# Two hybrid encoder layers: the decay mask on POOL, and reciprocal head norms issued ahead of their products

## The chip, the cores and the metric

The kernel runs on one core of a Trainium2 chip. The metric is the device time of one execution in microseconds (us), as the median of several runs. The engines are TensorE (PE, with its weight load PEld), VectorE (DVE), ScalarE (ACT), GpSimd (POOL) and SyncE (SP, which issues the DMAs here). Each engine works through its own instructions strictly in order and waits on semaphores for the others.

## What is computed

The reference runs two DeepNorm layers on x of 512 tokens by 1024 channels. A layer projects x once for three branches, merges them by gates and projects the sum back.

- **State space (SSD).** 32 heads in 4 groups, two directions, chunks of 128 tokens. A depthwise convolution over 5 taps acts on the inputs x, B and C. In each chunk the output is a product with a decay matrix, `decay = exp(where(lower, a_cum[q] - a_cum[s], -inf))`, added to what the earlier chunks left in the state; it is gated with SiLU(z) and normed.
- **Differential attention.** 8 heads, two softmax maps each, `A1 - lambda*A2` times V, then an RMS norm per head, `y * rsqrt(mean(y*y) + 1e-5) * w`, and a SiLU gate.
- **Cross attention** into 256 memory tokens, with a gate.

All of it is float32; the kernel splits float32 operands into a high and a low part, and makes three TensorE passes of each product.

## The kernel before, in words

Everything is laid out as channels on 128 partitions and 512 tokens along the row. Weights come in units of 128 x 1024: a DMA (`wr`), a high part on ACT (`wh`), a low part on DVE (`wl`), then 24 matmuls of 128x512 into a `pj` bank (8 slices of x, three passes each). A plan lists the jobs; a scheduler then orders the instructions of each engine by priorities. `late(n)` shifts the priority of what is issued inside it: a positive n later, a negative one earlier. A second device, a manual schedule on PE alone, keeps PE's instructions as written there.

**SSD (`ssd`, lines 416 to 634).** For each of the four groups the plan holds the B and C parts (projection, convolution, and for B a transpose `pt<-bC`), four x parts, the states, and then for each quarter b = 0 to 3 a z part and a y part. The B part of the next group follows straight after the y part of b = 3. A y part (line 500) does for each of its two heads:

- a DMA brings the cumulated exponents of both directions to all partitions, `ab` (512 KB; two buffers in all);
- line 524 puts the mask on them with VectorE, `min`, over 128 x 1024;
- ACT takes the exponential, eight instructions of 128x128, each with its own bias;
- DVE adds the two directions (`ab<-ab`) and multiplies with the B-C product of the group: `m<-ab,gs`;
- PE multiplies `m` with the transposed x (`pm<-m,xsT`, eight products for two heads, which are sixteen entries in the trace).

DVE then adds the inter-chunk part to `y`, multiplies with `sz` and splits y into `yh` (ACT) and `yl` (DVE). ACT squares it into `sz`, and POOL adds that to `sqa` (the only work that POOL has here, besides two memsets). The convolution (`conv`, line 400) begins with one ACT instruction that reads the projection's bank (`acc<-pj`), goes on with four DVE instructions (`acc<-pj,hcw,acc`), a tanh on ACT (`th<-acc`) and ends on DVE (for B: `bC<-th,acc`).

**Differential attention (`diff`, lines 785 to 1026).** 35 units are walked through with a step counter s = 0 to 34; nst = 32, and the last units are gates. At step s PE has the unit's 24 matmuls in two halves of 12, and around them the scores of step s + 1, the turning of step s, and the values. After the last head's values (s = 32) `sums` (PE, s = 33) makes the sum of squares of head 7, which ACT copies to `ss`. The function `norm` then makes the reciprocal norms on DVE: a reciprocal, three small operations, the `rsqrt` by Newton steps (twelve small operations, last written tile `rs_y`) and a product, all on 128x4 for one head. `norms` does this for heads 0 to 6 at s = 30 and sends the result through PE and ACT to DRAM (`rd`). `last` does it for head 7 in the middle of s = 33 and multiplies `rs_y` with an identity on PE, which spreads it over the partitions (`pm<-cst,rs_y`). `fin(h)` fetches a head's norms as a broadcast DMA (`fth<-rd`, two buffers; for head 7 it reads the `pm` bank), multiplies `sdy`, and splits the product into `dy` (ACT high part, DVE low part). Two heads are finished after each step from s = 31 on. After that `branch_out` multiplies `dy` with the output weights (24 matmuls for each of its units, `pj<-dy`).

Of the kernel before, what the change touches and what calls it, by code (L numbers as in the profile page):

```python
# [15 lines left out]
ALU = mybir.AluOpType  # L16
# [4 lines left out]
P = 128  # L21
S = 512
D = 1024
KC = D // P
NL = 2
M = 256
EPS = 1e-5
# [14 lines left out]

LX, LD = 70, 80

FILL = (0, 2, 0, 2, 0, 4, 0, 0)

# [3 lines left out]
def bc(ap, shape):  # L52
    return ap.broadcast_to(shape)


class Net:
# [359 lines left out]
    def ssd(self, l):  # L416
        nc = self.nc
# [78 lines left out]
        def ypart(g, b):  # L496
            def f():
                sp = self.sp
                if b == 0:
                    self.yh = self.t(sp, [P, 4, S], "yh", F32R)  # L500
                    self.yl = self.t(sp, [P, 4, S], "yl", F32R)

                eb = self.t(sp, [P, 2, S], "eb", bufs=2)
                for hh in range(2):
                    h = g * 8 + 2 * b + hh
                    src = self.deb.rearrange("(d h) q -> h d q", d=2)[h:h + 1]
                    nc.sync.dma_start(out=eb[hh * 64:(hh + 1) * 64], in_=src.broadcast_to([64, 2, S]))
                for d, cs in ((0, (1, 2, 3)), (1, (0, 1, 2))):
                    ps = self.bank(self.pm, "pm")
                    for c in cs:  # L510
                        q = slice(c * P, (c + 1) * P)
                        self.mm(ps[:, q], self.prev[d, c][:, b * P:(b + 1) * P], self.cC[:, q])
                    q = slice(cs[0] * P, (cs[2] + 1) * P)
                    self.tt(eb[:, d, q], ps[:, q], eb[:, d, q], ALU.mult)

                py = self.bank(self.pm, "pm")
                ms = []
                for hh in range(2):
                    h = g * 8 + 2 * b + hh
                    ab = self.t(sp, [P, 2, 4, P], "ab", bufs=2)  # L520
                    src = self.dab.rearrange("(d h) q -> h d q", d=2)[h:h + 1]
                    nc.sync.dma_start(out=ab.rearrange("p d c q -> p d (c q)"), in_=src.broadcast_to([P, 2, S]))

                    self.tt(ab, ab, bc(self.msk[:, :, None, :], [P, 2, 4, P]), ALU.min)
                    for d in range(2):
                        for c in range(4):
                            j = 32 * d + h
                            self.act(ab[:, d, c, :], ab[:, d, c, :], AF.Exp, bias=self.bias[:, c, j:j + 1])
                    self.tt(ab[:, 0], ab[:, 0], ab[:, 1], ALU.add)
                    m = self.t(sp, [P, 4, P], "m", bufs=3)  # L530
                    self.tt(m, ab[:, 0], self.gs, ALU.mult)
# [253 lines left out]
    def diff(self, l):  # L785
        nc = self.nc
# [131 lines left out]

        def norm(lo, hi):

            n = 4 * (hi - lo)
            s0, ss = self.s0[:, 4 * lo:4 * hi], self.ss[:, 4 * lo:4 * hi]
            nc.vector.reciprocal(out=s0, in_=s0)
            self.stt(ss, ss, 1.0 / 128.0, s0, ALU.mult, ALU.mult)
            self.tt(ss, ss, s0, ALU.mult)
            self.ts(ss, ss, EPS, ALU.add)
            r = self.rsqrt(self.fp, ss, n)
            self.tt(r, r, s0, ALU.mult)
            return r

        def norms():

            n = 4 * (KC - 1)
            r = norm(0, KC - 1)
            pt = self.bank(self.pt, "pt")
            self.tr(pt[:n, :P], r)
            rt = self.t(self.fp, [n, P], "rt", bufs=1)
            self.act(rt, pt[:n, :P])
            self.rd = self.t(self.dp, [n, P], "rd")
            nc.sync.dma_start(out=self.rd, in_=rt)  # L940

        def last():

            r = norm(KC - 1, KC)
            self.rb = self.bank(self.pm, "pm")
            for c in range(4):
                self.mm(self.rb[:, c * P:(c + 1) * P], bc(r[:, c:c + 1], [P, P]), self.ident)
# [12 lines left out]
        def step(unit, *parts):  # L960

            def f(wh, wl):
                g = fn(wh, wl)
                for p in parts:
                    for job in p:
                        job()
                    next(g, None)
            fn, u = unit
            self.T(f, u)

        def job(fn, *a):
            return lambda: fn(*a)
# [17 lines left out]
        nst = 4 * KC  # L990
        for s, unit in enumerate(units):
            first = [job(scores, s + 1)] if s + 1 < nst else []
            amid = []
            if s % 4 == 2 and s < nst:
                amid.append(job(values, s // 4, 0))
            if s % 4 == 0 and 0 < s <= nst:
                amid.append(job(values, s // 4 - 1, 1))
            if s < nst:
                amid.append(job(turn, s))
            if s % 4 == 1 and 1 < s <= nst + 1:  # L1000
                first.append(job(sums, s // 4 - 1))
            if s == nst - 2:
                amid.append(norms)
            if s == nst + 1:
                amid.append(last)
            step(unit, first, amid)
            if s >= nst - 1:
                for h in range(2 * (s - nst + 1), min(2 * (s - nst + 1) + 2, KC)):
                    self.T(job(fin, h))
        self.T(order.close)  # L1010
        mgs = ([], [])

# [216 lines left out]
```

## Time and profile before

| | |
|---|---|
| runs | 2237.81, 2241.68, 2244.03 us; median 2241.68 |
| the profiled execution | 2240.25 us, its span 2238.5 us |
| granted TensorE clock, mean | 0.994 |
| PE busy | 2173.2 us (97%) |
| DVE busy | 1589.9 us (71%) |
| ACT busy | 1004.6 us (45%) |
| POOL busy | 52.9 us (2%), 38 instructions |
| DMA | 283.79 MB, 127 GB/s |

A page's times are those of the one profiled execution. A row of the timeline gives the start, the duration, the engine and line, output and inputs, the shape, how many equal instructions were put together (x), and in square brackets how long the engine stood idle just before and what ended that. Matmuls overlap: a 128x512 matmul lasts 0.39 us, but the next one starts 0.23 us after it.

SSD of layer 0 lies at about 50 to 500 us, that of layer 1 at about 1200 to 1650 us. The end of the differential attention lies at about 1014 us and 2129 us.

### The profile page before, as it was taken

The page shows a single profiled execution, that of the slowest core. Times are in us where ns is not written, and L with a number is a line of the kernel's source. Part 1 is how long each engine was busy: PE and PEld are TensorE (multiplying, and loading weights), DVE is VectorE, ACT ScalarE, POOL GpSimd, SP SyncE. Part 2 cuts the span into 40 slices and gives each one's busy share as a digit, 9 for nine tenths or more (in the row PEclk, how much of TensorE's full clock was granted, in tenths as well). Part 3 has the DMA queues.
Part 4 walks back from the last instruction along what each step waited for, and adds up shares of the span by engine and source line. Part 5 has one row for each costly group of instructions (what it writes and reads, how often), then busy time and mean ns, then how long its engine had stood idle before and what let it go on. Part 6 is the DMA issues. An engine that isn't in the chain of part 4 may idle for free.

```text
span 2238.5 us, 30344 instructions
## 1 busy us (share of the span) xinstructions
PE 2173.2 (97%) x11714; PEld 1787.8 (80%) x11714; DVE 1589.9 (71%) x2468; ACT 1004.6 (45%) x1895; POOL 52.9 (2%) x38
## 2 busy tenths in 40 slices
PE   8999999999999999998999999999999999999898
PEld 6777877788888788877996777787788887888678
DVE  7887888758544777765567888888744547777657
ACT  5664545424432555442355564554423325544430
POOL 0000000000000000000000000010100000000000
PEclk9999999999999999999999999999999999999999
DMA  4654444425453222233564545453433332223333
GB/s 148 180 160 144 147 142 138 126 85 190 145 179 115 90 81 82 81 104 108 163 225 115 165 141 151 132 152 122 123 124 118 116 106 85 78 84 90 109 99 128
DMA packets 108278, 283.79 MB, mean 127 GB/s; under 512 B 12588, under 2 KB 17252, under 8 KB 107876
## 3 DMA queue, kind: packets, MB, share of 16 engines
q1 hardware_dynamic: 108132, 281.84, 41.2%
q8 instruction: 92, 1.51, 0.3%
q14 instruction: 54, 0.44, 0.1%
HBM read 255.55 MB, written 17.85 MB: 122 GB/s over the span
## 4 chain that ended last, share of the span: by engine, by line
PE 71%; DVE 14%; DMA 7%; ACT 5%; issue 2%; SPq 0%; POOL 0%; DVEq 0%; POOLq 0%; ACTq 0%
PE pj L103 59%; PE pm L103 9%; DMA ab<-dab 4%; DVE wl L81 2%; PE pt L111 2%; DVE ab L81 2%; DVE acc L84 2%; ACT ab L91 1%; ACT wh L91 1%; DVE y L81 1%; DVE rx L81 1%; PE pt L103 1%; DMA wr<-wu 1%; DMA fth<-rd 1%; DVE yl L84 1%
## 5 line engine op out<-in xcount | busy, mean ns | idle before, releaser
L103 PE MATMUL pj<-xh,wl 128*128 128x512 f32 x1664 | 669.1, 402 | 10.8 <-DVE wl L81 8.9
L103 PE MATMUL pj<-xh,wh 128*128 128x512 f32 x1664 | 660.8, 397 | 0.0
L103 PE MATMUL pj<-xl,wh 128*128 128x512 f32 x1664 | 658.1, 395 | 0.0
L81 DVE TENSOR_TENSOR wl<-wr,wh 128x1024 fp32r<-128x1024 f32 x330 | 404.5, 1226 | 108.3 <-ACT wh L91 107.5
L91 ACT ACTIVATE wh<-wr 128x1024 fp32r<-128x1024 f32 x330 | 347.4, 1053 | 235.3 <-PE pj L103 199.5
L103 PEld LDWEIGHTS pj<-xh,wl 128*128 128x128 f32 x1664 | 314.1, 189 | 90.8 <-issue 18.3
L103 PEld LDWEIGHTS pj<-xh,wh 128*128 128x128 f32 x1664 | 313.7, 189 | 71.6 <-issue 6.0
L103 PEld LDWEIGHTS pj<-xl,wh 128*128 128x128 f32 x1664 | 314.1, 189 | 63.5 <-issue 3.6
L91 ACT ACTIVATE ab<-ab,bias 128x128 f32<-128x128 f32 x512 | 160.7, 391 | 121.9 <-DVE ab L81 121.3
L84 DVE SCALAR_TENSOR_TENSOR acc<-pj,hcw,acc 128x510 f32<-128x510 f32 x192 | 142.4, 743 | 23.8 <-ACT acc L91 22.4
L91 ACT ACTIVATE fpp<-pm,fmx 128x512 f32<-128x512 f32 x128 | 87.9, 687 | 83.4 <-DVE fmx L881 82.6
L881 DVE TENSOR_REDUCE fmx<-pm 128x1 f32<-128x512 f32 x128 | 87.0, 686 | 45.4 <-PE pm L103 45.1
L103 PE MATMUL pj<-yl,wh 128*128 128x512 f32 x256 | 102.3, 400 | 0.8 <-DVE yl L84 0.8
L103 PE MATMUL pj<-yh,wh 128*128 128x512 f32 x256 | 103.1, 403 | 0.0
L81 DVE TENSOR_TENSOR ab<-ab,cst 128x1024 f32<-128x1024 f32 x64 | 86.3, 1349 | 22.9 <-DMA ab<-dab 22.8
L103 PE MATMUL pj<-dy,wh 128*128 128x512 f32 (+1 forms) x384 | 101.9, 354 | 0.0
L103 PE MATMUL pj<-yh,wl 128*128 128x512 f32 x256 | 101.9, 399 | 0.0
L103 PE MATMUL pj<-cy,wh 128*128 128x512 f32 x256 | 78.8, 389 | 0.0
L103 PEld LDWEIGHTS pj<-dy,wh 128*128 128x128 f32 x384 | 68.0, 189 | 10.0
L103 PE MATMUL pj<-wh,xl 128*128 128x256 f32 x256 | 74.8, 292 | 0.0
L103 PE MATMUL pj<-wl,xh 128*128 128x256 f32 x256 | 72.4, 283 | 0.0
L103 PE MATMUL pj<-wh,xh 128*128 128x256 f32 x256 | 72.3, 283 | 0.0
(273 smaller groups left out, 3387.3 us busy)
## 6 DMA issues: line engine op xcount, KB each, us to landing
wr<-wu SPq DMA_DIRECT2D x336, 512.0 KB, 3.6
ab<-dab SPq DMA_DIRECT2D x64, 512.0 KB, 5.7
eb<-deb SPq DMA_DIRECT2D x64, 256.0 KB, 4.8
mkv<-dkv SPq DMA_DIRECT2D x16, 512.0 KB, 4.3
rsw<-rx SPq DMA_DIRECT2D x128, 64.0 KB, 2.0
dgt<-tg SPq DMA_DIRECT2D x18, 256.0 KB, 2.6
dkv<-mo SPq DMA_DIRECT2D x16, 256.0 KB, 4.0
dkv<-q SPq DMA_DIRECT2D x16, 256.0 KB, 3.7
```

The costliest lines, as they stand in the source:

```text
L81: (eng or self.nc.vector).tensor_tensor(out=out, in0=a, in1=b, op=op)
L84: self.nc.vector.scalar_tensor_tensor(out=out, in0=a, scalar=s, in1=b, op0=op0, op1=op1)
L91: self.nc.scalar.activation(out=out, in_=a, func=f, **kw)
L103: self.nc.tensor.matmul(out=out, lhsT=a, rhs=b, start=first, stop=last)
L111: self.nc.tensor.transpose(out=out, in_=x, identity=self.ident)
L881: nc.vector.tensor_reduce(out=mx[:, c:c + 1], in_=ps, axis=AX.X, op=ALU.min)
```

## The change

Two edits.

1. The mask of the exponents, 64 instructions of 128 x 1024, moves from VectorE to GpSimd, and `min` becomes `add`.
2. In `diff`, `norm` is now a job of its own, with an earlier priority (`late(-300)`). For heads 0 to 6 it stands after step 29 and its result is spread at s = 30 as before. For head 7 it stands after step 33, and the product with the identity moves from the middle of s = 33 to the middle of s = 34. The `fin` jobs are dealt out otherwise: heads 0 and 1 after s = 32, heads 2 to 4 after s = 33, heads 5 to 7 after s = 34.

```diff
-LX, LD = 70, 80
+LX, LD, LN = 70, 80, 300
...
-                    self.tt(ab, ab, bc(self.msk[:, :, None, :], [P, 2, 4, P]), ALU.min)
+                    self.tt(ab, ab, bc(self.msk[:, :, None, :], [P, 2, 4, P]), ALU.add, nc.gpsimd)
...
         def norm(lo, hi):
-            n = 4 * (hi - lo)
             s0, ss = self.s0[:, 4 * lo:4 * hi], self.ss[:, 4 * lo:4 * hi]
-            nc.vector.reciprocal(out=s0, in_=s0)
...
-            r = self.rsqrt(self.fp, ss, n)
-            self.tt(r, r, s0, ALU.mult)
-            return r
+            with self.late(-LN):
+                nc.vector.reciprocal(out=s0, in_=s0)
...
+                self.r = self.rsqrt(self.fp, ss, 4 * (hi - lo))
+                self.tt(self.r, self.r, s0, ALU.mult)
-        def norms():
+        def spread():
             n = 4 * (KC - 1)
-            r = norm(0, KC - 1)
             pt = self.bank(self.pt, "pt")
-            self.tr(pt[:n, :P], r)
+            self.tr(pt[:n, :P], self.r)
...
         def last():
-            r = norm(KC - 1, KC)
+            r = self.r
...
             if s == nst - 2:
-                amid.append(norms)
-            if s == nst + 1:
+                amid.append(spread)
+            if s == nst + 2:
                 amid.append(last)
             step(unit, first, amid)
-            if s >= nst - 1:
-                for h in range(2 * (s - nst + 1), min(2 * (s - nst + 1) + 2, KC)):
-                    self.T(job(fin, h))
+            if s in (nst - 3, nst + 1):
+                self.T(job(norm, *((0, KC - 1) if s < nst else (KC - 1, KC))))
+            for h in {nst: (0, 1), nst + 1: (2, 3, 4), nst + 2: (5, 6, 7)}.get(s, ()):
+                self.T(job(fin, h))
```

The scheduler orders more than the edited lines. The first place is PE in layer 0, where group 1 ends and group 2 begins. `pm_1922` takes the products of the last quarter, `pj_2075` is the projection that follows, and `bC_1977` is group 2's convolved B. Before:

```order
L103 MATMUL pj_2075<-xl_83,wh_1973 128x512
L103 MATMUL pj_2075<-xh_82,wh_1973 128x512
L111 MATMUL pt_2012<-cst_81,bC_1977 128x128 x4
L103 MATMUL pj_2075<-xh_82,wl_1974 128x512
L103 MATMUL pj_2075<-xl_83,wh_1973 128x512
```

and in the changed kernel:

```order
L103 MATMUL pm_1922<-m_1949,xsT_1146 64x128
L103 MATMUL pm_1922<-m_1935,xsT_1146 64x128
L103 MATMUL pj_2075<-xh_82,wl_1974 128x512
L111 MATMUL pt_2012<-cst_81,bC_1977 128x128 x4
L103 MATMUL pj_2075<-xl_83,wh_1973 128x512
```

Before, 15 matmuls of `pj_2075` stand between the products `pm_1922` and the transposes of `bC_1977`; now one does. The same shift of 14 rows is there between groups 2 and 3, and at both places of layer 1. Between groups 0 and 1 the transposes stand 9 rows earlier (layer 0) and 12 (layer 1), and the products with `m` of group 0 stand 17 to 25 rows earlier in layer 0 and 17 to 45 in layer 1.

The second place is ACT at the same time. `ab_1937` is the last head of group 1, `ab_2483` the first of group 2, and `acc_2003` the convolution that becomes `bC_1977`; a minus is before, a plus is the changed kernel.

```order
 L91 ACTIVATE wh_1973<-wr_1971 128x1024
-L91 ACTIVATE ab_1937<-ab_1937,bias_358 128x128 x3
+L91 ACTIVATE ab_1937<-ab_1937,bias_358 128x128 x8
+L91 ACTIVATE ab_2483<-ab_2483,bias_358 128x128 x5
 L91 ACTIVATE yh_1546<-y_1830,pr_127 128x512
 L91 ACTIVATE sz_1775<-y_1830 128x512
-L91 ACTIVATE ab_1937<-ab_1937,bias_358 128x128 x5
+L91 ACTIVATE ab_2483<-ab_2483,bias_358 128x128 x3
 L91 ACTIVATE acc_2003<-pj_1978,hcw_131 128x512
 L91 ACTIVATE wh_2021<-wr_2019 128x1024
-L91 ACTIVATE ab_2483<-ab_2483,bias_358 128x128 x8
```

The eight exponentials of `ab_2483` stood behind the convolution's first instruction and now stand ahead of it; `yh` and `sz` moved from between the exponentials of `ab_1937` to between those of `ab_2483`.

The third place is PE at the end of the differential attention of layer 1. `rs_y` holds head 7's reciprocal norms, `pj_18545` is the unit of s = 33, `pj_18603` (before: `pj_18613`) that of s = 34, and `pj_18657` the first output product, which reads `dy`. Before:

```order
L103 MATMUL pj_18545<-xl_83,wh_18427 128x512
L103 MATMUL pj_18545<-xh_82,wh_18427 128x512
L103 MATMUL pm_18578<-cst_81,rs_y_18562 128x128 x4
L103 MATMUL pj_18545<-xh_82,wl_18428 128x512
L103 MATMUL pj_18545<-xl_83,wh_18427 128x512
```

and in the changed kernel:

```order
L103 MATMUL pj_18657<-dy_2627_15727,wh_18525 128x512
L103 MATMUL pj_18657<-dy_2626_15726,wh_18525 128x512
L103 MATMUL pj_18657<-dy_2626_15726,wl_18526 128x512
L103 MATMUL pm_18616<-cst_81,rs_y_18566 128x128 x4
L103 MATMUL pj_18603<-xh_82,wl_18468 128x512
```

Between the sums of head 7 and the product with `rs_y` there stood 12 matmuls; now there are 46: all 24 of s = 33, 12 of s = 34, and 10 of the first output product, which need the finished heads 0 to 3.

More of the change, by code (lines that the diff above doesn't have):

```diff
@@ L919, in norm @@
         def norm(lo, hi):
-            n = 4 * (hi - lo)
             s0, ss = self.s0[:, 4 * lo:4 * hi], self.ss[:, 4 * lo:4 * hi]
-            nc.vector.reciprocal(out=s0, in_=s0)
-            self.stt(ss, ss, 1.0 / 128.0, s0, ALU.mult, ALU.mult)
-            self.tt(ss, ss, s0, ALU.mult)
-            self.ts(ss, ss, EPS, ALU.add)
-            r = self.rsqrt(self.fp, ss, n)
-            self.tt(r, r, s0, ALU.mult)
-            return r
-        def norms():
+            with self.late(-LN):
+                nc.vector.reciprocal(out=s0, in_=s0)
+                self.stt(ss, ss, 1.0 / 128.0, s0, ALU.mult, ALU.mult)
+                self.tt(ss, ss, s0, ALU.mult)
+                self.ts(ss, ss, EPS, ALU.add)
+                self.r = self.rsqrt(self.fp, ss, 4 * (hi - lo))
+                self.tt(self.r, self.r, s0, ALU.mult)
+        def spread():
             n = 4 * (KC - 1)
-            r = norm(0, KC - 1)
             pt = self.bank(self.pt, "pt")
-            self.tr(pt[:n, :P], r)
+            self.tr(pt[:n, :P], self.r)
             rt = self.t(self.fp, [n, P], "rt", bufs=1)
```

## The prediction

> **What bounds the kernel now.** I read the page first (span and engines), then the table of windows over the state space stage, then the table of waits, and then the timeline at the two kinds of place that the change touches.
>
> ```profile
> span 2238.5 us, 30344 instructions
> PE 2173.2 (97%) x11714; PEld 1787.8 (80%) x11714; DVE 1589.9 (71%) x2468; ACT 1004.6 (45%) x1895; POOL 52.9 (2%) x38
> ```
>
> PE is busy for 2173.2 of 2238.5 us, so the kernel is bound by PE, and only 65 us of idle PE and some time at a lowered clock can be won. Anything that makes PE wait is lost at once. The state space stage of layer 0, in windows (PE, PEld, DVE, ACT and POOL busy, granted clock, DMA):
>
> ```profile
> 50.00:100.00 50.00, 46.59 (x242) 35.50 (x241) 43.87 (x65) 31.54 (x71) 1.54 (x1) 1.00 0.64 168
> 100.00:150.00 50.00, 47.96 (x247) 39.42 (x246) 47.10 (x61) 32.74 (x71) 4.41 (x3) 1.00 0.63 179
> 150.00:200.00 50.00, 50.00 (x237) 38.53 (x236) 35.33 (x49) 23.70 (x48) 0.00 (x0) 1.00 0.34 101
> 200.00:250.00 50.00, 49.80 (x267) 40.09 (x267) 47.85 (x63) 27.98 (x58) 6.23 (x4) 1.00 0.59 181
> ```
>
> Group 0 (to about 130 us) leaves PE idle for 3.4 and 2.0 us of 50, with DVE at 44 and 47. From 150 us on PE has no idle time, although DVE is at 48 of 50 between 200 and 250 us. A freer DVE can therefore win only in group 0; later it only adds slack. The waits that matter here:
>
> ```profile
> DVE ab L81 <- DMA ab<-dab: 22.8, 21, 2.5
> PEld pm L103 <- DVE rs_y L81: 17.0, 2, 8.6
> PE pm L103 <- DVE rs_y L81: 16.1, 2, 8.2
> PE pm L103 <- DVE m L81: 8.8, 7, 1.9
> ```
>
> PE waits 16.1 us for `rs_y` at two places (once in each layer), and 8.8 us in seven waits for `m`, which are those of group 0. The first is what edit 2 addresses. The second, and a DVE that waits 22.8 us for the exponents' DMA, is where edit 1 has its say.
>
> **Edit 2, the reciprocal norms.** The timeline of PE at the end of layer 1's differential attention: sums of head 7, the last of the 12 matmuls behind them, the product with `rs_y`, the first one after it, the first at full pace, and the first and last rows of the first output product:
>
> ```profile
> 2117.61 0.95 PE L103 MATMUL pt<-cst,fth 128*128 128x1 f32 x8
> ...
> 2121.04 0.39 PE L103 MATMUL pj<-xh,wh 128*128 128x512 f32 x1
> 2129.38 2.08 PE L103 MATMUL pm<-cst,rs_y 128*128 128x128 f32 x8 [7.96 <-DVE rs_y L81]
> 2131.11 0.77 PE L103 MATMUL pj<-xh,wl 128*128 128x512 f32 x1
> ...
> 2134.12 0.40 PE L103 MATMUL pj<-xl,wh 128*128 128x512 f32 x1
> ...
> 2140.74 0.39 PE L103 MATMUL pj<-dy,wl 128*128 128x512 f32 x1
> ...
> 2145.50 0.39 PE L103 MATMUL pj<-dy,wl 128*128 128x512 f32 x1
> 2145.73 0.61 PE L103 MATMUL pj<-dy,wh 128*128 128x512 f32 x2
> ```
>
> Between 2140.74 and 2145.50 lie 21 matmuls, 0.227 us each; that is PE's pace. From 2121.43 to the end of the first output product at about 2146.2 there are 24.8 us. The work in them is 12 + 24 + 24 matmuls, 13.6 us, and the four products with `rs_y`. Those took 1.73 us (2129.38 to 2131.11) at the clock of this window:
>
> ```profile
> 2125.00:2130.00 5.00, 0.62 (x3) 0.62 (x4) 3.67 (x14) 1.26 (x2) 0.00 (x0) 0.50 0.19 68
> ```
>
> At the granted 0.50 they cost 1.73, so 0.9 at full clock. Lost are 24.8 - 13.6 - 0.9 = 10.3 us: 7.96 of idle time, and 2.3 of matmuls at a lowered clock (0.50 here; the seven between 2131.11 and 2134.12 took 0.43 us each).
>
> The Trainium skill's "TensorE: Matmul & The Clock Gate" (Part 1) says that an idle activity window, some 3.4 us by its figure, halves the clock until PE has been busy for about as long; the 0.50 after 7.96 idle us agrees.
>
> What fills that hole now: DVE, on which the Newton steps and the heads' `fin` interleave, and the fetches of the norms.
>
> ```profile
> 2118.09 0.69 DVE L81 TENSOR_TENSOR sdy<-sdy,fth 128x512 f32<-128x512 f32 x1 [1.64 <-DMA fth<-rd]
> 2121.79 0.69 DVE L81 TENSOR_TENSOR sdy<-sdy,fth 128x512 f32<-128x512 f32 x1 [0.49 <-DMA fth<-rd]
> ...
> 2127.18 0.68 DVE L81 TENSOR_TENSOR sdy<-sdy,fth 128x512 f32<-128x512 f32 x1
> ...
> 2129.17 0.16 DVE L81 TENSOR_TENSOR rs_y<-rs_y,fs 128x4 f32<-128x4 f32 x1
> ```
>
> In the new order PE has 34 more matmuls between the sums and `rs_y`: 7.7 us, which bring it from 2121.3 to 2129.0. The chain to `rs_y` keeps its neighbours on DVE (five `fin` products are still woven into it), so I leave its end at 2129.2 to 2129.8: PE waits up to 0.8 us, and not long enough for the clock. The ten output matmuls in front of it need heads 0 to 3; the fourth of those, by the rows above, is multiplied at about 2127 and split 1.3 us later, before the tenth matmul (2128.8). A late fetch there costs 1 us at most. So of 10.3 us 8.5 to 9.3 are won in layer 1. In layer 0 the wait is 8.2 (the longest in the table), with the same rows around it. I take 8.5 each: **-17 us**, bounds -20.6 (nothing left of the hole) and -11 (the fetches, which start a step later, push `rs_y` 3 us behind).
>
> Moving `norm` for heads 0 to 6 ahead costs nothing: PE does not wait for that one now, and DVE has idle time beside it. SP gets no new DMA; the fetches for heads 0 and 1 stand one step later in its queue, which the bound above covers.
>
> **Edit 1, the cost of a mask.** Before, from the views of the tiles `ab` and `sqa`, min/median/max in ns:
>
> ```profile
> L81 DVE TENSOR_TENSOR ab<-ab,cst x64: 1207/1220/2342, 65.5 to 1600.2; 128x1024 f32<-128x1024 f32 x64
> ...
> L81 POOL TENSOR_TENSOR sqa<-sqa,sz x32: 1289/1524/2664, 91.1 to 1613.9; 128x512 f32<-128x512 f32 x32
> ```
>
> DVE loses 64 x 1.22 us, 39 us per layer. POOL takes at least 1.289 us for half the width, so a mask takes between 1.29 (all overhead) and 2.6 us (none) unhindered, and up to 5.3 by the slowest row. I take 2.5, near twice the fastest row, since 1024 elements a partition leave little to overhead. POOL is at 2% and has room; what counts is that each head's chain (DMA, mask, exponentials, sum, `m`) grows by 1.3 us. The "GPSIMD Engine Reference" of the Trainium skill (3.1) has 4497 ns for an add of 2048 elements against 2293 on VectorE; by it the estimate for a mask is 2.25, and the sum below would be 1 us smaller.
>
> **Edit 1, what it does to others.** At 224.9 us POOL and DVE, each with two inputs from SBUF, ran into one another:
>
> ```profile
> 224.91 1.30 POOL L81 TENSOR_TENSOR sqa<-sqa,sz 128x512 f32<-128x512 f32 x1 [11.94 <-ACT sz L91]
> ```
>
> ```profile
> 208.13 1.23 DVE L81 TENSOR_TENSOR ab<-ab,cst 128x1024 f32<-128x1024 f32 x1 [0.29 <-DMA ab<-dab]
> ...
> 217.60 0.69 DVE L81 TENSOR_TENSOR m<-ab,gs 128x512 f32<-128x512 f32 x1
> ...
> 221.34 1.22 DVE L81 TENSOR_TENSOR ab<-ab,cst 128x1024 f32<-128x1024 f32 x1
> ...
> 224.94 2.34 DVE L81 TENSOR_TENSOR ab<-ab,cst 128x1024 f32<-128x1024 f32 x1
> ...
> 228.47 0.68 DVE L81 TENSOR_TENSOR m<-ab,gs 128x512 f32<-128x512 f32 x1
> ...
> 234.55 0.68 DVE L84 SCALAR_TENSOR_TENSOR bC<-th,acc 128x512 f32<-128x512 f32 x1
> ```
>
> The mask that began 0.03 us behind POOL's addition took 2.34 instead of 1.22: it stood still until POOL ended. So 64 masks of 2.5 us on POOL can stop DVE for up to as long as DVE is relieved, and DVE can stop them. The Trainium skill's "SBUF — State Buffer" ("Who interferes with whom") calls this an exclusive lock on a shared port pair for the whole instruction, when DVE reads two SBUF inputs and GpSimd reads SBUF; the 2.34 agrees, and it speaks against the change.
>
> **Edit 1, where PE waits.** PE at the end of group 1 in layer 0, and the three other places of the same kind:
>
> ```profile
> 230.70 1.09 PE L103 MATMUL pm<-m,xsT 128*64 128x128 f32 x16
> ...
> 235.29 0.66 PE L111 MATMUL pt<-cst,bC 128*128 128x128 f32 x4
> ```
>
> ```profile
> 342.82 0.66 PE L111 MATMUL pt<-cst,bC 128*128 128x128 f32 x4
> ```
>
> ```profile
> 1398.69 0.55 PE L111 MATMUL pt<-cst,bC 128*128 128x128 f32 x3 [0.77 <-DVE bC L84]
> ```
>
> `bC` ends at 234.55 + 0.68 = 235.23, and PE takes it at 235.29: it is just in time already, at 1398.69 it is late. In the new order PE asks for it 14 matmuls earlier, 3.2 us, at about 232.1. So `bC` would have to end 3 us sooner than now. Does it? ACT before:
>
> ```profile
> 224.67 1.56 ACT L91 ACTIVATE ab<-ab,bias 128x128 f32<-128x128 f32 x5
> 226.13 0.76 ACT L91 ACTIVATE acc<-pj,hcw 128x512 f32<-128x512 f32 x1
> ...
> 227.75 2.43 ACT L91 ACTIVATE ab<-ab,bias 128x128 f32<-128x128 f32 x8
> ```
>
> The convolution began on ACT at 226.13, ahead of the next group's exponentials; now it stands behind them. Their data came by 224.94, the mask on POOL ends at 224.94 + 2.5 = 227.4, and then come five exponentials (1.56), `yh` and `sz` (1.3) and three more (0.9): the convolution starts at 231.2, 5 us later than before. The rest of it took 235.23 - 226.13 = 9.1 us, with a sum, an `m` and parts of `y` woven in that no longer stand there (5 instructions of about 0.6): 5.8 us remain, so `bC` ends at 237.0 and PE waits 237.0 - 232.1 = **4.9 us**. If POOL were as fast as DVE it would be 3.6; one collision of 1.1 us on each engine makes it 7. Nothing behind the place gives it back, since PE has no idle time there to shrink. Four such places: 4 x 5 = **+20**, bounds 0 and +28.
>
> Between groups 0 and 1, `bC` is asked for 9 and 12 matmuls earlier, 2.0 and 2.7 us; I take **+5** for both, bounds 0 and +10. In group 0 the products with `m` are asked for 17 to 45 matmuls earlier (3.9 to 10 us), DVE has 8 x 1.22 us less to do, and the chains are 1.3 us longer. The 8.8 us of waits there may vanish or double: **0**, bounds -9 and +9. Each stall may lower the clock: 0.77 us did nothing visible and 7.96 us cost 2.3, so 0 to 2.3 for each of four; I take 0.5 each: **+2**.
>
> Sum: -17 + 20 + 5 + 0 + 2 = **+10 us**. The profiled execution's own time is 2240.25 us (its span, and 1.75 around it), 1.4 under the median of the runs; on the median of 2241.7 the forecast is **2251 us**.
>
> **The rivals.**
>
> *The freer DVE carries it (faster).* If the exponent chain runs ahead, with `ab` masked early enough, `bC` meets the new order. It decides at one point: the mask of `ab_2483` must end by about 222.5, so that `bC` ends by 232.1. For it: DVE at 48 of 50 in that window, so all that waits in DVE's queue comes sooner. Against it: the data land 5.7 us after their buffer comes free, which the next row shows, and `ab_2483` needs the buffer of a head whose `m` ended at 218.3.
>
> ```profile
> DMA to landing us min/median/max: 4.7/5.7/10.7
> ```
>
> Then only the -17 is left: 2225. Chance 0.26.
>
> *A draw.* The stalls at `bC` are there but half as long (2.5 us each, 10), groups 0 and 1 add 5, the clock stays: 2240. Chance 0.21.
>
> *POOL becomes the late engine (much slower).* If masks and DVE's two-input instructions stop one another throughout, a mask takes 3.6 us and each head's chain 2.4 more, `m` is late too in groups 1 to 3, and stalls of 7 us come with a lowered clock: 28 + 10 + 4 - 17, to 2267. Chance 0.15. For it: 2.34 and 2664 ns above. Against it: the convolution's instructions and the first of `y` read a PSUM bank, and from 208.13 to 221.34 there are two masks in 13 us.
>
> *The hole in the tail stays.* If the fetches hold up heads 0 to 3, PE waits ahead of the output products instead. By the order `rs_y` does move; else the sum is +27, and 2269. Chance 0.04. The forecast has the rest, 0.34.
>
> **How the numbers follow.** About 0.3% (6.7 us) is what a measurement of this kernel can tell from no change. Slower by more: forecast, POOL late, hole stays, 0.53, less a little of the forecast that ends within 6 us: 0.51. Within: the rest of the draw and that little, 0.22. Faster: the first rival and the draw's lowest end, 0.27. The range leaves out the best of the first rival and the worst of the third: 2223 to 2270; for the forecast alone it is 2246 to 2259.
>
> **What would show it.** The wait of PE for `rs_y` shrinks from 16.1 to under 2 us, and the clock around the tail stays at 1.00. POOL has 64 masks of about 2.5 us. PE waits for `bC` at four places for 3 to 7 us, and the `acc<-pj` in front of it starts 4 us or more later than the products with `m` allow. If those waits are missing while the masks last 2.5 us, the step on the convolution's place behind the exponentials is wrong; if a mask takes under 1.5 us, its price is; if the tail wins under 5 us per layer, the count of matmuls there is.

## The result, and the profile after

The changed kernel takes 2341.67 us (median of 5 runs, 2340.22 to 2346.06), the kernel before 2242.17 us (5 runs). The ratio is 1.0449, with a 95% interval of 1.0433 to 1.0465: 99.5 us slower, where 2251 us and a range of 2223 to 2270 had been forecast. The sign was right and the size was not. Of the four runs of `e15_eighth` below one took 6532 us, and the median given for it is that of the other three.

The page of the changed kernel:

```profile
span 2344.3 us, 30504 instructions
PE 2207.2 (94%) x11714; PEld 1812.7 (77%) x11714; DVE 1573.3 (67%) x2404; ACT 1005.5 (43%) x1895; POOL 218.3 (9%) x102
```

The span grew by 105.8 us. PE is busy 34.0 us longer with the same 11714 instructions, so a third of the loss is PE at a lower clock (0.976 in the mean, 0.994 before); the rest is waits. By landmarks that every trace has (the first `pt<-cst,sqa` of a layer's state space, the transpose of the norms of heads 0 to 6, layer 1's first `pt<-cst,bC`), the stages took, in us:

| stage | before | changed | mask on VectorE (below) |
|---|---|---|---|
| start to the end of layer 0's state space | 451.8 | 511.1 | 450.3 |
| on to the norms of heads 0 to 6 | 534.5 | 537.9 | 534.9 |
| on to layer 1's first `bC` | 194.6 | 186.5 | 185.5 |
| on to the end of its state space | 434.8 | 493.5 | 431.4 |
| on to the norms of heads 0 to 6 | 486.2 | 487.1 | 487.1 |
| on to the end | 136.6 | 128.1 | 127.4 |

Edit 2 does what was forecast: the two stages with the ends of the differential attention are 8.1 and 8.5 us shorter. The two state space stages are 59.3 and 58.7 us longer. The waits of PE after:

```profile
PE pt L111 <- DVE bC L84: 46.5, 7, 9.1
PE pm L103 <- DVE m L81: 20.5, 14, 4.5
PE pj L103 <- DVE mrg L81: 13.9, 6, 3.3
PE pj L103 <- ACT mrg L91: 9.6, 4, 3.5
PE pm L103 <- DVE xw L81: 8.7, 3, 4.0
PE pm L103 <- DVE rs_y L81: 1.9, 2, 1.1
```

The wait for `rs_y` went from 16.1 to 1.9. The one for `bC` is the largest, as forecast, but 46.5 instead of some 25; `m` is waited for 14 times instead of 7, and the merge (`mrg`, where the last group's output products hand over their banks) costs 23.5, against 1.9 before.

The place that the prediction worked through, the end of group 1 in layer 0. PE (products with `m`, transposes of `bC`), then POOL, ACT and DVE:

```profile
253.82 1.09 PE L103 MATMUL pm<-m,xsT 128*64 128x128 f32 x16
263.27 1.11 PE L111 MATMUL pt<-cst,bC 128*128 128x128 f32 x4 [7.91 <-DVE bC L84]
```

```profile
249.51 2.40 POOL L81 TENSOR_TENSOR ab<-ab,cst 128x1024 f32<-128x1024 f32 x1 [0.86 <-DMA ab<-dab]
254.79 1.80 POOL L81 TENSOR_TENSOR sqa<-sqa,sz 128x512 f32<-128x512 f32 x1 [2.88 <-ACT sz L91]
260.32 2.35 POOL L81 TENSOR_TENSOR ab<-ab,cst 128x1024 f32<-128x1024 f32 x1 [3.73 <-DMA ab<-dab]
```

```profile
251.95 1.57 ACT L91 ACTIVATE ab<-ab,bias 128x128 f32<-128x128 f32 x5 [0.81 <-POOL ab L81]
253.43 0.71 ACT L91 ACTIVATE yh<-y,pr 128x512 fp32r<-128x512 f32 x1
254.04 0.61 ACT L91 ACTIVATE sz<-y 128x512 f32<-128x512 f32 x1
254.56 0.97 ACT L91 ACTIVATE ab<-ab,bias 128x128 f32<-128x128 f32 x3
255.44 0.76 ACT L91 ACTIVATE acc<-pj,hcw 128x512 f32<-128x512 f32 x1
```

```profile
255.62 1.52 DVE L81 TENSOR_TENSOR ab<-ab 128x512 f32<-128x512 f32 x1 [0.16 <-issue]
257.06 1.52 DVE L84 SCALAR_TENSOR_TENSOR acc<-pj,hcw,acc 128x510 f32<-128x510 f32 x2
258.50 1.21 DVE L81 TENSOR_TENSOR wl<-wr,wh 128x1024 fp32r<-128x1024 f32 x1
259.63 1.53 DVE L84 SCALAR_TENSOR_TENSOR acc<-pj,hcw,acc 128x511 f32<-128x511 f32 x2
261.91 1.30 DVE L84 SCALAR_TENSOR_TENSOR bC<-th,acc 128x512 f32<-128x512 f32 x1 [0.76 <-ACT th L91]
```

One reads it from the end: PE stood from 255.4 to 263.27 for `bC`. The convolution began on ACT at 255.44, behind the five, two and three instructions that the new order put ahead of it, and those waited for POOL's mask (to 251.91). On its way through DVE it was stopped twice: the sum `ab<-ab` took 1.52 us instead of 0.68 while POOL added `sqa`, and `bC` took 1.30 instead of 0.68 behind the mask at 260.32. The windows behind the wait show what it does to the clock (granted clock before the DMA's two columns):

```profile
255.00:260.00 5.00, 0.36 (x1) 0.04 (x1) 4.81 (x6) 2.15 (x4) 1.59 (x1) 1.00 0.70 210
260.00:265.00 5.00, 1.73 (x6) 1.58 (x7) 4.21 (x6) 2.82 (x5) 2.35 (x1) 0.52 0.37 110
265.00:270.00 5.00, 5.00 (x19) 4.05 (x18) 5.00 (x9) 4.14 (x12) 0.22 (x1) 0.80 0.27 84
```

### The profile page after: what moved, and what is told of

Its sections match the earlier page's. It is cut to its first block, busy times and chain, and to the rows that moved or that the text cites. A ratio compares the mean times of both kernels' runs of the same rounds, so it can differ in the third digit from the quotient of the medians.

```text
span 2344.3 us, 30504 instructions
## 1 busy us (share of the span) xinstructions
PE 2207.2 (94%) x11714; PEld 1812.7 (77%) x11714; DVE 1573.3 (67%) x2404; ACT 1005.5 (43%) x1895; POOL 218.3 (9%) x102
## 4 chain that ended last, share of the span: by engine, by line
PE 61%; DVE 14%; DMA 10%; ACT 8%; POOL 3%; issue 2%; SPq 0%; POOLq 0%; DVEq 0%; ACTq 0%
PE pj L103 50%; PE pm L103 7%; DMA ab<-dab 6%; POOL ab L81 3%; DVE wl L81 3%; ACT ab L91 3%; PE pt L111 2%; DVE acc L84 2%; ACT wh L91 1%; DVE y L81 1%; DVE ab L81 1%; DVE rx L81 1%; DMA fth<-rd 1%; DVE m L81 1%; PE pt L103 1%
## 5 line engine op out<-in xcount | busy, mean ns | idle before, releaser
L103 PE MATMUL pj<-xh,wl 128*128 128x512 f32 x1664 | 678.2, 408 | 32.0 <-DVE mrg L81 13.9
L103 PE MATMUL pj<-xl,wh 128*128 128x512 f32 x1664 | 669.9, 403 | 0.0
L103 PE MATMUL pj<-xh,wh 128*128 128x512 f32 x1664 | 669.6, 402 | 0.0
L81 DVE TENSOR_TENSOR wl<-wr,wh 128x1024 fp32r<-128x1024 f32 x330 | 418.1, 1267 | 100.9 <-ACT wh L91 100.3
L103 PEld LDWEIGHTS pj<-xh,wl 128*128 128x128 f32 x1664 | 319.2, 192 | 117.2 <-issue 17.7
L103 PEld LDWEIGHTS pj<-xh,wh 128*128 128x128 f32 x1664 | 320.0, 192 | 73.8 <-issue 5.8
L103 PEld LDWEIGHTS pj<-xl,wh 128*128 128x128 f32 x1664 | 320.4, 193 | 65.8 <-issue 4.3
L81 POOL TENSOR_TENSOR ab<-ab,cst 128x1024 f32<-128x1024 f32 x64 | 161.3, 2522 | 445.2 <-DMA ab<-dab 414.1
L81 POOL TENSOR_TENSOR sqa<-sqa,sz 128x512 f32<-128x512 f32 x32 | 55.8, 1745 | 356.1 <-ACT sz L91 356.0
L81 DVE TENSOR_TENSOR ab<-ab 128x512 f32<-128x512 f32 x64 | 57.4, 896 | 43.3 <-ACT ab L91 33.7
```

Of the source, the lines that this page charges most:

```text
L81: (eng or self.nc.vector).tensor_tensor(out=out, in0=a, in1=b, op=op)
L103: self.nc.tensor.matmul(out=out, lhsT=a, rhs=b, start=first, stop=last)
```

## The experiments

The theory after this reading: the loss is edit 1's alone, and has three parts: the **order** (PE asks for `bC` too soon, and the convolution stands behind the next head's exponentials), the **collision** (POOL and DVE stop one another), and the **chain** (each head's mask takes 1.2 us longer on POOL). The rivals: that one of them is all of it. Times below are differences of medians to the kernel before, run in the same job (2239.5 to 2241.8 us).

### Edit 1 alone, and the mask on VectorE

`e2_mask_alone` is the kernel before with line 524 changed and `diff` left as it was. 

> Only edit 1 (the mask as an addition on POOL), with the end of the differential attention as before. Between the landmarks of the two traces the state space stages grew by 59.3 and 58.7 us and the ends of the differential attention shrank by 8.1 and 8.5. If the two edits add up, this kernel takes 2341.7 + 16.6 = 2358 us (plus or minus 3), with PE waiting for rs_y 16 us again. If the second edit's early priorities disturb the state space stage as well, it takes clearly less.

Measured: 2359.37 us, ratio 1.0518 (1.0493 to 1.0543), +117.5. The two edits add up to within 4 us: 117.5 less the 21.8 that edit 2 wins in the next run is 95.7, and the changed kernel lost 99.5. PE waits for `rs_y` as before:

```profile
PE pm L103 <- DVE rs_y L81: 17.0, 2, 8.9
```

`e3_add_on_dve` is the changed kernel with one argument taken away:

```diff
-self.tt(ab, ab, ..., ALU.add, nc.gpsimd)
+self.tt(ab, ab, ..., ALU.add)
```

> Edit 2 in full, and the mask as an addition, but on VectorE: the only thing undone is the engine of the mask. If the loss is all POOL's, it takes 2242.2 - 16.6 = 2225.6 us (plus or minus 3), with masks of 1.22 us as with min and waits for rs_y of 2 us in all. If the addition itself or the second edit has a part in the loss, it is slower than 2235.

Measured: 2220.03 us, ratio 0.9906 (0.9886 to 0.9925), -21.8. It is the fastest version of this study. The addition costs DVE what the minimum did:

```profile
PE 2171.7 (98%) x11714; PEld 1786.8 (81%) x11714; DVE 1589.5 (72%) x2468; ACT 1004.6 (45%) x1895; POOL 53.6 (2%) x38
...
L81 DVE TENSOR_TENSOR ab<-ab,cst 128x1024 f32<-128x1024 f32 x64 | 87.0, 1359 | 18.0 <-DMA ab<-dab 17.8
```

So moving the mask to POOL costs 121.6 us, and edit 2 wins 21.8, of which, in the one profiled execution of each kernel, 9.2 lie in each of the two stages with the ends of the differential attention and 3.4 in layer 1's state space. These two rows also show where DVE's relief went. Without the masks DVE would be busy 1589.5 - 87.0 = 1502.5 us; in the changed kernel it is 1573.3. Of 87 us of relief 71 came back in DVE's other instructions, which took longer.

### The collision by itself

`e4_pool_beside` has the mask on VectorE, and in each quarter, ahead of POOL's addition:

```diff
+for _ in range(3):
+    sv = self.sqa.rearrange("p (c q) -> p c q", c=4)
+    self.tt(sv, sv, bc(self.ones[:, None, :], [P, 4, P]), ALU.mult, nc.gpsimd)
 self.tt(self.sqa, self.sqa, sq, ALU.add, nc.gpsimd)
```

> As the kernel with the addition on VectorE, and in each quarter POOL also multiplies sqa by ones three times (three 128x512 instructions, about 4.6 us, where two masks would take 4.8), which no other engine waits for. It measures what POOL's reading beside VectorE costs when no chain runs through POOL. Theory 'collision' (the shared access to SBUF makes the loss): 60 us or more over the kernel without the three, since POOL is as busy as in the changed kernel. Theory 'chain and order' (the masks are late for what PE asks for): under 15 us.

Measured: 2277.40 us, ratio 1.0156 (1.0140 to 1.0172), +35.6: 57 us over the mask on VectorE, though no other engine waits for the three products. That is just under the 60 that the theory of the collision asked for, and far over the 15 of the other. PE waits for `m` 20 times instead of 6. The timeline shows how, POOL first (the last quarter's addition, then three products) and then DVE:

```profile
221.61 1.30 POOL L81 TENSOR_TENSOR sqa<-sqa,sz 128x512 f32<-128x512 f32 x1 [3.85 <-ACT sz L91]
222.98 5.54 POOL L81 TENSOR_TENSOR sqa<-sqa,cst 128x512 f32<-128x512 f32 x3
```

```profile
221.65 2.34 DVE L81 TENSOR_TENSOR ab<-ab,cst 128x1024 f32<-128x1024 f32 x1
223.91 1.78 DVE L81 TENSOR_TENSOR ab<-ab 128x512 f32<-128x512 f32 x1
225.72 1.66 DVE L81 TENSOR_TENSOR m<-ab,gs 128x512 f32<-128x512 f32 x1
227.31 2.29 DVE L81 TENSOR_TENSOR wl<-wr,wh 128x1024 fp32r<-128x1024 f32 x1
229.52 0.68 DVE L81 TENSOR_TENSOR ab<-ab 128x512 f32<-128x512 f32 x1
```

As long as POOL works, each DVE instruction takes 1.0 to 1.1 us more, in turns with POOL's; the next one after it takes its usual 0.68. That is the collision: four POOL instructions here, and four DVE instructions held up, in a stage where DVE had no time to spare (47.85 of 50 us busy in the kernel before).

`e12_copy1_pool` and `e13_copy2_pool` repeat it with a DVE that is relieved of the masks; they are told below, with the kernels they are built on.

### The order

`e5_bc_order` leaves the masks on POOL and has PE ask later for `bC`:

```diff
-LX, LD, LN = 70, 80, 300
+LX, LD, LN, LB, LC = 70, 80, 300, 120, 150
...
-self.conv(self.proj(wh, wl), 16 + g, self.bC)
+ps = self.proj(wh, wl)
+with self.late(-LC):
+    self.conv(ps, 16 + g, self.bC)
...
+with self.late(LB):
+    for c in range(4):
+        self.tr(pt[:, c * P:(c + 1) * P], self.bC[:, c * P:(c + 1) * P])
```

> The changed kernel with the transposes of bC put later by priority 120 and the convolution of the B part earlier by 150: PE asks for bC 25 or more matmuls later than in the changed kernel, while the masks stay on POOL and ACT keeps its order. Theory 'order': the six long waits for bC (44 us) go, and with them the low clock behind each (about 2.3 us each), so 2342 - 58 = 2284, or up to 20 less if the waits for the merge come from them too. Theory 'chain or collision': the waits move to the next thing on the chain, and it wins under 20 us.

Measured: 2331.56 us, ratio 1.0403 (1.0378 to 1.0428), +89.7. It wins 10 of 121. The long waits for `bC` are gone, and in their stead PE waits for `yh`, which needs `y`, which needs the products with `m`, the end of the same chain:

```profile
PE pj L103 <- ACT yh L91: 20.0, 6, 5.4
```

Asking later for one thing on a late chain only finds the next. The order as sole cause falls.

`e7_copy1` and `e8_copy2` take the mask away from POOL and DVE. They leave the mask out and cut the bias at 0; ACT copies `ab` onto itself, once or twice:

```diff
-self.tt(ab, ab, ..., ALU.add, nc.gpsimd)
+self.act(ab, ab)
```

> The changed kernel without any mask; in its place ACT copies ab onto itself (128x1024, 1.05 us by the weight's copy of that size). It leaves the mask out and cuts the bias at 0 so that the exponentials stay finite. VectorE is relieved as in the changed kernel, POOL reads nothing more than before, the chain is as long as with the mask on VectorE, and PE asks for bC as early as in the changed kernel. Theory 'order': it still loses most, over 2280. Theories 'chain' and 'collision': at or under the 2220 of the mask on VectorE, since nothing collides and the chain is no longer; the relief of VectorE should show as the waits of group 0 that go, 2210-2220.

Measured: 2255.32 us, ratio 1.0067 (1.0045 to 1.0089), +15.1: slower than with the mask on VectorE by 37 us, although DVE is relieved, POOL has nothing but its additions to `sqa`, and the chain is no longer. Neither half of the expectation was met: an order alone costs something, but a third. And the order is not the changed kernel's, though the expectation took it for that: between groups 1, 2 and 3 PE has 10 rows between the products with `m` and the transposes of `bC`, where the kernel before has 15 and the changed kernel one.

> As the one before with two copies on ACT one after another, 2.1 us in place of POOL's mask of 2.4: nearly the changed kernel's chain, with VectorE relieved and without POOL's reading. Theory 'chain': most of the loss is there, 2300 or more. Theory 'collision': under 2240, the rest being ACT's 64 x 2.1 us that stand ahead of other work. If chain and collision share the 122 us about evenly: 2270.

Measured: 2235.65 us, ratio 0.9979 (0.9969 to 0.9989), -4.6: with a longer chain and 67 us more on ACT it is 20 us *faster* than with one copy. The waits for `bC`, with one copy and with two:

```profile
PE pt L111 <- DVE bC L84: 23.5, 7, 5.2
```

```profile
PE pt L111 <- DVE bC L84: 9.9, 7, 2.4
```

At the four places between groups 1, 2 and 3 PE asks for `bC` at the same row in both; it waits there 17.8 us with one copy and 5.7 with two. What differs there is ACT. With one copy the next group's copy and four of its exponentials stand ahead of the convolution's first instruction, which starts at 236.92, 1.44 us before the products with `m` (238.36):

```profile
236.92 0.77 ACT L91 ACTIVATE acc<-pj,hcw 128x512 f32<-128x512 f32 x1
```

With two copies the convolution stands ahead of them; it starts at 234.73, 3.13 us before them (237.86):

```profile
234.73 0.76 ACT L91 ACTIVATE acc<-pj,hcw 128x512 f32<-128x512 f32 x1
```

The convolution's other end differs too. With one copy its tanh stands on ACT behind the copy of a later head, and that copy waits for the exponents' DMA. DVE had ended its part at 242.34, and the tanh began 2.6 us later:

```profile
241.60 0.74 DVE L84 SCALAR_TENSOR_TENSOR acc<-pj,hcw,acc 128x510 f32<-128x510 f32 x1
```

```profile
242.88 1.06 ACT L91 ACTIVATE ab<-ab 128x1024 f32<-128x1024 f32 x1 [3.07 <-DMA ab<-dab]
...
244.94 0.62 ACT L91 ACTIVATE th<-acc 128x512 f32<-128x512 f32 x1
```

At the four places the tanh is late by 8.5 us in all with one copy and by 0.8 with two, which is most of the 12.1 us by which PE's waits there differ. In the changed kernel it is not late at these places (0.1 us each).

So an order costs about 37 us with one copy and 17 with two, what the relief of DVE wins already taken off. The place of the convolution on ACT, its first instruction and its tanh, is the likeliest reason for the difference; other rows of the two kernels differ as well, and it is not shown to be the only one. What the changed kernel's own order costs, neither of the two measures.

Now the same two kernels with POOL's three products beside them. 

> The kernel with one ACT copy for the mask (2255 us), and POOL's three products per quarter beside it: the changed kernel's order and relief of VectorE, POOL as busy, but no head's chain goes through POOL. It leaves the mask out and cuts the bias at 0. If the costs add up, 2255 + 57 = 2312, and what is missing to 2342 (30 us) is the chain through POOL. If a relieved VectorE takes the collisions without loss, it stays under 2275, and the changed kernel's loss lies in the chain through POOL (some 70 us). If order and collision make each other worse, 2330 or more.

> The kernel with two ACT copies for the mask (2236 us; the convolution of B starts on ACT ahead of the next group's exponentials), and POOL's three products per quarter beside it. It leaves the mask out and cuts the bias at 0. If the costs add up, 2236 + 57 = 2293. If the 57 us came from a VectorE that had no room for them, a VectorE relieved of 78 us hides most: under 2260.

Measured: 2281.35 us, ratio 1.0196 (1.0175 to 1.0217), +41.9; and 2264.29 us, ratio 1.0113 (1.0095 to 1.0131), +24.8. The products cost 27 and 29 us here, half of the 57 that they cost beside a loaded DVE. A relieved DVE takes half of the collisions without loss, not all: neither the plain sum of the costs (2312 and 2293) nor the full hiding (under 2275 and 2260) came out. With one copy and the products, DVE is busy as long as in the changed kernel:

```profile
PE 2191.6 (96%) x11714; PEld 1802.3 (79%) x11714; DVE 1573.8 (69%) x2406; ACT 1066.8 (47%) x1959; POOL 214.0 (9%) x134
```

So the same 71 us of relief came back on DVE, and yet this kernel loses 58 us less than the changed one: how long DVE is held up in all does not settle the loss. Which of its instructions are held up, and who waits for them, must count as well. If the changed kernel's order costs what this one does, order and collision make 64 of 121 us, and 58 are left.

### The size of the mask

`e6_split` gives half of each mask to each engine:

```diff
-self.tt(ab, ab, ..., ALU.add, nc.gpsimd)
+for d, eng in ((0, nc.gpsimd), (1, nc.vector)):
+    self.tt(ab[:, d], ab[:, d], ..., ALU.add, eng)
```

> The changed kernel with the mask divided: the first direction (128x512) on POOL, the second on VectorE. Both halves can run at the same time, so a mask is done after about 1.3 us when they do not stand in each other's way, as long as the whole one on VectorE took, and POOL reads half as long. Theory 'chain' (the loss comes from the 1.2 us by which the mask on POOL is longer): back to 2220-2230 us. Theory 'collision': half of what the three products beside VectorE cost, 2220 + 29 = 2249, or more, since the two halves collide with each other. Both together: about half of 122, so 2280.

Measured: 2304.58 us, ratio 1.0287 (1.0255 to 1.0319), +64.4. It is slower than each theory alone gave, and than both together (2280), though a mask is done about as soon as on VectorE when both halves run freely (POOL's half takes 1.26 us at the fastest, a whole one on VectorE 1.22).

`e14_half` and `e15_eighth` keep only a part of the mask, on POOL: one direction, and one block of one direction. They leave the rest out and cut the bias at 0. On PE, ACT and DVE both have the same order as each other. It is near the changed kernel's on PE, where the transposes of `bC` stand one row later between groups 1, 2 and 3; on ACT it differs at more places.

```diff
-self.tt(ab, ab, ..., ALU.add, nc.gpsimd)
+self.tt(ab[:, 0], ab[:, 0], bc(self.msk[:, 0:1, :], [P, 4, P]), ALU.add, nc.gpsimd)
```

```diff
-self.tt(ab, ab, ..., ALU.add, nc.gpsimd)
+self.tt(ab[:, 0, 0], ab[:, 0, 0], self.msk[:, 0], ALU.add, nc.gpsimd)
```

> The changed kernel with POOL masking the first direction only (128x512, about 1.3-1.6 us instead of 2.4); the other direction is left unmasked and the bias is cut at 0. Order nearly as in the changed kernel. If the loss goes with POOL's time (collisions 26 us for 150 us of POOL, the chain's 60 us for 1.35 us per head): order 35, collisions 14, chain 10-15, so 2220 + 62 = 2282. If going through POOL costs by itself, whatever the size: 2315 or more. If only the order counts: 2255.

> As the one before with POOL masking one block of 128x128 only; the same order on PE and ACT as with half the mask, instruction by instruction. The difference of the two is POOL's time alone. If the loss goes with POOL's time: the order's 35 us remain, or less, since the chain is now shorter than with VectorE's mask: 2245-2255. If a hop through POOL costs by itself: 2290 or more.

Measured: 2300.42 us, ratio 1.0274 (1.0253 to 1.0294), +59.5; and 2271.69 us, ratio 1.0145 (1.0125 to 1.0166), +30.7. Both lie between what was expected of a loss that goes with POOL's time (2282, and 2245 to 2255) and of a price for each hop through POOL (2315, and 2290). POOL's masks in the eighth, the half and the whole:

```profile
L81 POOL TENSOR_TENSOR ab<-ab,cst 128x128 f32<-128x128 f32 x64 | 39.9, 624 | 453.5 <-DMA ab<-dab 359.1 <-DMA eb<-deb 64.0 <-DVE eb L81 10.4
```

```profile
L81 POOL TENSOR_TENSOR ab<-ab,cst 128x512 f32<-128x512 f32 x64 | 91.4, 1428 | 443.8 <-DMA ab<-dab 406.5 <-DVE y L84 10.8 <-DVE eb L81 7.5
```

```profile
L81 POOL TENSOR_TENSOR ab<-ab,cst 128x1024 f32<-128x1024 f32 x64 | 161.3, 2522 | 445.2 <-DMA ab<-dab 414.1 <-ACT wh L91 11.6 <-DVE eb L81 7.0
```

From 39.9 to 91.4 us of masks the time grows by 28.8, from 91.4 to 161.3 by 40.0: 0.56 and 0.57 us for each us of mask on POOL. The first step is between two kernels of one order, so it is POOL's time alone that costs it. Drawn back to none it is 52.5 - 0.56 x 39.9 = 30 us over the mask on VectorE; by the intervals of the two ratios this estimate is good to some 9 us. The kernel with one copy gave 37, in another order, so that the two are of one size but do not prove each other. `e6_split` lies on the same line, 30 + 0.56 x 101.0 us of POOL's masks is 87, measured 86; its order is its own and its VectorE keeps half of each mask, so this is weak support.

The estimate, then: some 30 to 37 us for the order, which are there however short the mask is, and some 84 to 91 that go with POOL's time. Of those some 27 are collisions, by the kernels with POOL's products outside the chain. The remaining 60 or so are what POOL's time costs for being in the chain; that is a difference of runs whose orders are not equal, and it is less sure than the other two. It holds masks that end later and collisions on the chain itself, and no run here separates these. Length alone is not shown to cost it: with two copies the chain is nearly as long (2.1 us for the mask's 2.4), and that kernel takes 2236 us, in an order of its own. What grows from the half mask to the whole is not the wait for `bC` (47.9 and 46.5 us) but those for `m` (7.9 and 20.5) and the merge (12.8 and 23.5).

One rival was not tried: a third buffer for `ab`. On the chain that ended last, as the pages have it, the DMA of `ab` makes 6% of the span in the changed kernel and 4% with the mask on VectorE; a later mask frees its buffer later.

### Group 0 only

`e9_group0` has the mask on POOL where VectorE was the bound, and on VectorE in groups 1 to 3:

```diff
-..., ALU.add, nc.gpsimd)
+..., ALU.add, nc.gpsimd if g == 0 else None)
```

> The changed kernel with the mask on POOL in group 0 only (16 of 64 masks) and as an addition on VectorE elsewhere. Group 0 is where VectorE was the bound. If relief of VectorE is worth something anywhere, it is here: faster than 2220. If collision and chain cost as much per mask as in the other groups: 2220 + 122/4 = 2250.

Measured: 2251.63 us, ratio 1.0044 (1.0033 to 1.0055), +11.4, so 33 us over the mask on VectorE, for a quarter of the masks: by and large the equal price per mask (2250), and not the gain. PE's waits for `m` and `xw`, group 0's own, are longer, not shorter (7.0 and 2.5 with all masks on VectorE):

```profile
PE pm L103 <- DVE m L81: 15.9, 6, 4.0
PE pm L103 <- DVE xw L81: 10.3, 3, 6.2
```

So the relief does not pay even in the group where VectorE was the bound. The other groups were not measured alone.

## Why the prediction was wrong, point by point

- **The tail, -17.** Right. The wait of PE for `rs_y` fell to 1.9 us, the stages shrank by 16.6 us in the changed kernel and 18.4 with the mask on VectorE. PE reaches the product 11.5 us after the start of the sums (11.4 by the forecast's count) and waits 1.11 us:

```profile
2231.88 0.95 PE L103 MATMUL pt<-cst,fth 128*128 128x1 f32 x8
...
2244.51 1.16 PE L103 MATMUL pm<-cst,rs_y 128*128 128x128 f32 x8 [1.11 <-DVE rs_y L81]
```

- **The price of a mask, 2.5 us.** Right: 2.40 in the median, 2.52 in the mean.

- **The place, 4.9 us.** Right in its mechanism, short in size. The convolution starts 1.6 us after PE's products with `m` instead of 4.6 before them, 6.2 us later; 5 was forecast. From there to `bC` it took 7.8 us, where 5.8 was counted (five instructions of 0.6 us less than 9.1 are 6.1, so the count itself was a little short); 1.5 of the 2.0 us come from the two collisions shown above. The prediction had one such collision only in its upper bound. The waits at the four places are 7.9, 9.1, 8.6 and 7.8, and 5.8 and 4.9 between groups 0 and 1 where 2.5 each was taken. In all 46.5 for 25. That the kernel with one copy waits 23.5 us for `bC`, near the forecast, is chance: its order is another, and part of its wait is the tanh behind the copy.

- **Other waits, 0.** Wrong, and this is one half of the step that failed: the sum let PE wait at the `bC` of each group and nowhere behind it, and these other waits were 42 us. It waits longer for `m` (+11.7), `xw` (+5.2), the merge (+21.6) and `sqa` (+3.7). Only the waits of group 0 had a term (0, bounds -9 and +9); there `m` grew by 6.2 and `xw` by 5.4. The other 31 us had none. "Nothing behind the place gives it back, since PE has no idle time there to shrink" is true, but it asks only what could shrink. Behind the wait for `bC` at 263.27 PE waits again, 3.29 us for the merge at 291.92, and so after the other groups. The likely reason is that DVE came out of each stop late as well; that is argued from the rows and not tested by itself.

- **The clock, +2.** Wrong by most: PE was busy 34.0 us longer. The prediction took half a microsecond for each of four waits, between 0.77 us with no loss and 7.96 us with 2.3. There were 22 waits over 2 us, where the kernel before has four; after the one of 7.91 us shown above the window's clock was 0.52, then 0.80. The price was too low as well. The trace of the kernel before has a wait between the two that the prediction did not use, 2.48 us long, with a clock of 0.66 in the 5 us behind it, an estimated 1.7 us lost:

```profile
1226.09 3.62 PE L103 MATMUL pm<-xw,bT 128*128 128x512 f32 x4 [2.48 <-DVE xw L81]
```

```profile
1226.00:1231.00 5.00, 4.91 (x9) 2.39 (x10) 3.81 (x8) 3.46 (x9) 0.00 (x0) 0.66 0.94 198
```

In the two profiled executions these are all of it. In PE's waits and busy time, changed minus before: `bC` 44.0, `m` 11.7, `xw` 5.2, merge 21.6, `sqa` 3.7, clock 34.0, `rs_y` -14.2; together 106.0, and the span grew by 105.8.

- **The relief of DVE.** The other half of the step that failed. The prediction set the relief (39 us per layer) against collisions "for up to as long as DVE is relieved", and left both out of the sum in groups 1 to 3. The bound was there and was nearly reached, 71 of 87 us, and it was given no price. What the runs showed in its place: POOL's reading costs 57 us beside a loaded DVE and 27 beside a relieved one when no chain runs through POOL, and the masks in the chain cost some 60 more. How these 60 come about stays open, as said above. The rival "POOL becomes the late engine" had part of the mechanism, with 15 in 100, and 2267 us. The stalls of 7 us with a lowered clock came; but its masks of 3.6 us did not (2.52 in the mean, so it was DVE that was held up and hardly POOL), `m` outside group 0 makes only 5.5 us of waits, and its clock term was again only 4 us.

The Trainium skill's "SBUF — State Buffer" ("Who interferes with whom") says that a DVE instruction with two inputs from SBUF contends with a GpSimd instruction that reads SBUF, and that one with at most one such input does not, outside DVE's two-port modes. The means at the end of this document agree. The prediction cited it for one row and did not follow it through the stage.

## What to carry to other kernels

An engine with 2% of load is not free capacity if its reads hold up the loaded engine, as POOL's held up DVE's here. Before counting the relief, count each instruction moved to it as one instruction of the other engine held up, over the whole stage, and ask which of those lie on a chain that PE waits for: the same 71 us on DVE went with a loss of 42 us in one kernel and of 99 in another. In a kernel bound by PE, price the waits with the clock that follows: here 86 us of added waits came with 34 us of matmuls at a lower clock. And moving one step reorders the others: look at what now stands behind it on every engine, above all behind a step that waits for a DMA.

## What the runs showed of the hardware

- Which DVE instructions POOL's reading holds up. Means with the masks on VectorE and on POOL, both inputs in SBUF: `y<-y,sz` 684 and 1231 ns, `bC<-th,acc` 680 and 1428, `ab<-ab` 698 and 896. One input in PSUM: `eb<-pm,eb` 553 and 554 ns, `acc<-pj,hcw,acc` 742 and 744. The last two, in the changed kernel:

```profile
L84 DVE SCALAR_TENSOR_TENSOR acc<-pj,hcw,acc 128x510 f32<-128x510 f32 x192 | 142.9, 744 | 93.1 <-ACT acc L91 91.3
...
L81 DVE TENSOR_TENSOR eb<-pm,eb 128x384 f32<-128x384 f32 x64 | 35.5, 554 | 7.5 <-PE pm L103 6.8 <-issue 0.2
```

- POOL's addition goes with its width: 0.46 us for 128x128, 1.30 for 128x512 and 2.40 for 128x1024 (medians), about 0.2 us and 2.15 ns an element per partition; DVE takes 1.22 us for 128x1024.
